# Gate rows from TensorE instead of a trip through DRAM, and a later, smaller write of the bias vectors

## The chip, the cores and the metric

The kernel runs on one core of a Trainium2 chip. The metric is the device time in microseconds (us) of one execution. Engines are named TensorE (PE in the rows; PEld is its weight load), VectorE (DVE), ScalarE (ACT), GpSimd (POOL) and SyncE (SP). A `q` behind an engine's name (ACTq, SPq) marks what its sequencer issues, DMAs above all.

## What is computed

Two layers of a decoder on 512 tokens of width 1024, float32, with a conditioning vector `c`:

```python
c_act = silu(c)
for l in range(2):
    ada = c_act @ ada_w[l] + ada_b[l]
    sh1, sc1, g1, sh2, sc2, g2 = split(ada, 6)
    h = x * (1 + sc1) + sh1
    y = even_mixer(h) if l == 0 else diff_mixer(h)    # attention; all logits get a relative-position bias
    x = layer_norm(ALPHA * x + (1 + g1) * y, ln_g[l, 0], ln_b[l, 0])
    h = x * (1 + sc2) + sh2
    y = square(relu(h @ w1[l])) @ w2[l]
    x = layer_norm(ALPHA * x + (1 + g2) * y, ln_g[l, 1], ln_b[l, 1])
```

The even mixer has eight heads of sparse attention (compressed, selected and window branches) and eight heads over a latent with a top-k selection; the odd mixer is differential attention. The relative-position bias comes from a table of 32 buckets by 16 heads and depends on the distance alone. The four vectors `1 + g1`, `1 + g2` of the two layers are what this case calls the gates.

## The kernel before

Tokens are cut into four tiles of 128, the width into eight pieces of 128. Weights come as 512 KB loads on SyncE's queue, in a fixed order, into a few raw buffers (`raw`, `early`, `s`); ScalarE casts each to a high part (L265), VectorE or GpSimd makes the low part (L266), and a product is three matmuls (L350 to L352). The instructions of every engine are put in order ahead of time by a program that goes by priority, which is the order of the code, and by its own estimate of times; an engine then runs its list in that order and waits where an input is late. PSUM has eight banks, two for each of the tags `mm`, `s`, `t` and `o`.

*Conditioning.* `adac` holds the conditioning vectors as columns (128 partitions, eight pieces). Those of the first projection come in pairs (shift and scale of piece k) from loads `ada_w` multiplied and summed on VectorE (L250) or on GpSimd and ScalarE (L247, L248).

*Gates.* A gate multiplies either the rows of an output-projection weight (L262) or the MLP's sum (L824), so it is needed as a row of 1024 repeated on 128 partitions: the tile `grow`, of which there is one buffer for all four. `gate_row(l, i)` scales the column on VectorE (L984) and calls `row` (L430), which sends the column to DRAM as a vector (L435, 1024 elements of 4 bytes) and loads it from there onto all partitions (L440, 512 KB). Both DMAs are issued by ScalarE, and the second waits for the first. Calls: for (0,0) in the loop of the sparse attention, for (0,1) in the first MLP behind the first halves of its six whole-width products (`gemm1`), for (1,0) behind the value projection of the second layer, and for (1,1) in the second MLP as in the first. Since the order of work follows what is ready, the column of (0,1) goes out while layer 0's first LayerNorm still runs (L663 is that LayerNorm's square root on ScalarE, L706 its transposes on TensorE), that of (1,0) at 631.8 us, and that of (1,1) at 779.3 us, near the end of the first MLP. There, behind it on ScalarE's queue, stands the load of `subln` (L1595, 128 floats on all partitions), a constant of the second layer that VectorE scales (L1623) between the last groups of the first MLP.

*Bias vectors.* `bias_vectors` (L587) makes, by a one-hot product, a vector of 640 biases for each of 16 heads, and a second one for the compressed branch (8 heads, 1056 values). `write` sends them to DRAM, the first in `NREP` = 35 copies of 2,560 bytes (L606, one DMA of 1400 KB), the second in 8 copies (L608, two DMAs), all on ScalarE's queue. `gtile` (L533) later reads a tile of 128 rows by 512, each row shifted by one, out of these copies (L537, SyncE's queue). The write stands in the first projection's loop over the pieces k of the width: it is issued behind the activation of piece k = 6 (L1051). That loop casts a piece's weights (L265), makes the modulated input's high and low part (L1051 to L1053) and multiplies.

Of the kernel before, what the change touches and what calls it, by code (L numbers as in the profile page):

```python
# [9 lines left out]
F32 = mybir.dt.float32  # L10
# [13 lines left out]
NVEC = 640  # L24
# [4 lines left out]
def f32(ap):  # L29
    return ap.bitcast(F32)  # L30
# [46 lines left out]
 'cp': (),  # L77
 'd4': (22, 26, 37, 46),
 'cu': {(0, 0): 3, (0, 1): 4, (0, 2): 6, (0, 3): 7, (1, 0): 16, (1, 1): 17, (1, 2): 20, (1, 3): 21}}
NREP = 35  # L80


class Part:


    def __init__(self, *tiles):
        self.tiles = tiles
# [239 lines left out]
class Trunk:  # L327
    def __init__(self, tc, a, out):
        self.tc, self.nc, self.a, self.out = tc, tc.nc, a, out
        self.lo_engine = "vector"  # L330
        self.n_rows, self.marks, self.last_max = 0, {}, None
        self.ada_tag = "mm"
        self.slotm, self.phase = {}, None
        self.sums, self.site = {}, 0
        self.st = Stream(self)
        self.gate, self.w1, self.w2, self.wp = {}, {}, {}, {}
        self.xd, self.xr = {}, {}
        self.groups = [(0, 1, 2), (3, 4, 5)] + [(f, f + 1) for f in range(6, 28, 2)] + [(28, 29, 30, 31)]
# [91 lines left out]
    def row(self, col, pool, tag, bufs=1):  # L430

        nc = self.nc
        self.n_rows += 1
        d = self.DR.tile([1024], F32, name=f"row{self.n_rows}")
        nc.scalar.dma_start(out=d.rearrange("(k p) -> p k", p=128), in_=col)  # L435
        return self.row_in(d, pool, tag, bufs)

    def row_in(self, src, pool, tag, bufs=1):
        r = pool.tile([128, 1024], F32, tag=tag, bufs=bufs, name=tag)
        self.nc.scalar.dma_start(out=r, in_=src[None, :].to_broadcast([128, 1024]))  # L440
        return r

    def proj_q(self, ps, it, c0, c1, k):
# [89 lines left out]
    def gtile(self, col):  # L533

        g = self.s2("g")
        b = self.bvec[col]
        self.nc.sync.dma_start(out=g, in_=bass.AP(tensor=b.tensor, offset=b.offset + 127,  # L537
                                                  ap=[[NVEC - 32, 4], [NVEC - 1, 32], [1, 512]]))
        return g


# [45 lines left out]
    def bias_vectors(self):  # L587
# [5 lines left out]
        for i in range(2):  # L593
            nc.scalar.dma_start(out=oh[i], in_=a["onehot"][:, HB * i:HB * i + HB])
        self.bvec = self.DR.tile([16, NREP, NVEC], F32, name="bvec")
        self.bdec = self.DR.tile([8, 8, 16 * NDEC], F32, name="bdec")
# [8 lines left out]
        def write():  # L605
            nc.scalar.dma_start(out=self.bvec, in_=sb[0][:, None, :NVEC].to_broadcast([16, NREP, NVEC]))  # L606
            for x, c in ((sb[0][:8, NVEC:], slice(0, HB - NVEC)), (sb[1][:8], slice(HB - NVEC, 16 * NDEC))):
                nc.scalar.dma_start(out=self.bdec[:, :, c], in_=x[:, None, :].to_broadcast([8, 8, x.shape[1]]))  # L608
# [181 lines left out]
    def mlp(self, l, acc, rows, last):  # L790

        nc, st = self.nc, self.st
        h1, turn = {}, [0]
        self.ada_tag = "s"

        def relu2(ps, c0, c1, hh, hl):
            r = self.z()[:, :c1 - c0]
# [232 lines left out]
    def even(self):  # L1030
        nc, a, sm, R, B, st, I = self.nc, self.a, self.sm, self.R, self.B, self.st, self.I
# [13 lines left out]
        for k in range(8):  # L1045
            st.get(I["ada", k, True])
            c2 = self.adac[:, 0, 0:16].rearrange("p (s k) -> p k s", k=8)[:, k]
            b2 = self.adab[:, 0, 0:16].rearrange("p (s k) -> p k s", k=8)[:, k]
            nc.vector.tensor_add(out=mod[:, k], in0=c2, in1=b2)
            x = xs[k].rearrange("p (t c) -> p t c", t=4)  # L1050
            act = nc.scalar.activation(out=hh[:, :, k], in_=x, func=AF.Identity, scale=mod[:, k, 1:2], bias=mod[:, k, 0:1])  # L1051
            nc.vector.tensor_scalar(out=x, in0=x, scalar1=mod[:, k, 1:2], scalar2=mod[:, k, 0:1], op0=ALU.mult, op1=ALU.add)
            nc.vector.tensor_sub(out=hl[:, :, k], in0=x, in1=f32(hh[:, :, k]))  # L1053
            w = st.get(I["b1", k])
            for n in range(4):
                self.mm3(ps1[n], [y.cols(128 * n, 128) for y in w], (hh[:, :, k], hl[:, :, k]), k == 0, k == 7)
            for t in range(4):
                self.mm3(ps1[4 + t][:, :416], (hh[:, t, k], hl[:, t, k]), [y.cols(512, 416) for y in w], k == 0, k == 7)
            st.free(I["b1", k])
            if 1 and k == 6:  # L1060
                with self.tc.issue_after(act.ins):
                    bias_write()

# [20 lines left out]
        for t in range(4):  # L1084
            ps, ts = ps1[4 + t], slice(128 * t, 128 * t + 128)
# [45 lines left out]
        due, d = {}, 1 << 30  # L1131
        for x in reversed(PLAN["ord"]):
            d = due[x] = min(d, X0 + PLAN["due"][x] if x in PLAN["due"] else d)
# [244 lines left out]
        for t in range(4):  # L1378
            ps = self.bank("mm")
# [208 lines left out]
    def odd(self):  # L1588
        nc, a, sm, R, B, C, st, I = self.nc, self.a, self.sm, self.R, self.B, self.C, self.st, self.I
# [10 lines left out]
        for half in range(2):  # L1600
            V[half] = [self.s4() if half else B.tile([128, 1024], F32, tag="u4", bufs=4, name="V") for _ in range(2)]
            for t in range(4):
# [3 lines left out]
                ps = self.bank("mm")  # L1606
# [14 lines left out]
        nc.vector.tensor_sub(out=lf[:, 2:3], in0=lf[:, 0:1], in1=lf[:, 1:2])  # L1621
        nc.vector.tensor_scalar_add(out=lf[:, 2:3], in0=lf[:, 2:3], scalar1=LAMBDA_INIT)
        nc.vector.tensor_scalar_mul(out=sub, in0=sub, scalar1=1.0 - LAMBDA_INIT)  # L1623
        self.gate_row(1, 0)
        self.mark("o")

# [295 lines left out]
```

## Time and profile before

| | |
|---|---|
| three runs | 1472.17, 1480.51, 1480.96 us; median 1480.51 |
| profiled execution | 1476.66 us, span 1474.6 us |
| mean granted TensorE clock | 0.958 of full |
| busy | TensorE 1338.9, VectorE 1144.8, ScalarE 655.6, GpSimd 577.6 us |
| DMA | 192.09 MB, of which SyncE's ring (q1) 184.67 and ScalarE's ring (q10) 5.98 |

How the rows further down are read. A timeline row has the start in us from the span's beginning, the duration in us, the engine, the line of the code, the operation with out<-in, shapes and count; brackets at its end give how long the engine had stood idle before it and what ended that. A chain row has start, duration and what the last-ending chain of work consisted of there: an engine's work, or a DMA from its issue to its landing. A row of stretches has the stretch, its length, each engine's busy time (with the number of instructions), then the granted TensorE clock, the share of time in which the 16 DMA engines were busy, and GB/s. A row of groups has line, engine, operation, shape and count, then the busy time and the mean in ns, then idle time before. A row of one line's instructions has duration as least/median/most in ns, then first and last start in us. A row of DMA rings has packets, MB and the share of the 16 engines' time in the stretch.

### The profile page before, as it was taken

The numbers are of one execution on the slowest core, as the hardware profiler recorded it, in microseconds if no ns is written. First come the engines' busy times: TensorE is split into PE (matmuls) and PEld (weight loads), VectorE is DVE, ScalarE is ACT, GpSimd is POOL, SyncE is SP. The second block draws the span as 40 slices with busy tenths as digits, with TensorE's granted clock in tenths as the row PEclk, the third lists the DMA queues.
The fourth block names the chain that finished last, engine by engine and source line by source line (L and its number), as shares of the span: only waits on it lengthen the run. The fifth ranks groups of instructions, "written<-read, shape, count | busy, mean of one in ns | idle before, by whom it ended". The sixth has DMA issues, their size and how long they took to land.

```text
span 1474.6 us, 22436 instructions
## 1 busy us (share of the span) xinstructions
PE 1338.9 (91%) x8222; PEld 1117.6 (76%) x8222; DVE 1144.8 (78%) x2185; ACT 655.6 (44%) x1404; POOL 577.6 (39%) x432
## 2 busy tenths in 40 slices
PE   6859889999879999999997799999969899999995
PEld 4738667677569888878886678887759789999974
DVE  6577898866576787878787934778965988988898
ACT  2344456746444433323332425777565433333321
POOL 2151368745441353534444531124252632222244
PEclk9969899999989999999998999999989999999997
DMA  9943433322660445373534343233341233223311
GB/s 333 232 142 117 137 101 103 130 97 72 233 185 12 172 158 207 136 205 138 208 141 103 127 171 114 93 95 100 128 149 53 72 115 112 76 99 115 113 60 58
DMA packets 63427, 192.09 MB, mean 130 GB/s; under 512 B 11875, under 2 KB 12579, under 8 KB 63317
## 3 DMA queue, kind: packets, MB, share of 16 engines
q1 hardware_dynamic: 55712, 184.67, 37.6%
q10 hardware_dynamic: 7604, 5.98, 2.0%
q8 instruction: 65, 1.06, 0.3%
q14 instruction: 46, 0.37, 0.1%
HBM read 180.52 MB, written 10.11 MB: 129 GB/s over the span
## 4 chain that ended last, share of the span: by engine, by line
PE 67%; DVE 19%; DMA 7%; issue 3%; ACT 3%; POOL 0%; DVEq 0%; ACTq 0%; SPq 0%; POOLq 0%
PE ps_mm L350 9%; PE ps_mm L351 8%; PE ps_mm L352 8%; PE ps_o L350 4%; PE ps_o L351 4%; PE ps_o L352 4%; PE ps_s L350 3%; PE ps_s L351 3%; PE ps_s L352 3%; DVE b L266 2%; PE ps_t L352 2%; PE ps_t L350 2%; PE ps_t L351 2%; DMA raw<-ev_b 2%; PE ps_s L422 2%
## 5 line engine op out<-in xcount | busy, mean ns | idle before, releaser
L350 PE MATMUL ps_mm<-hT,b 128*128 128x256 f32 (+1 forms) x560 | 190.1, 342 | 21.6 <-ACT b L265 13.2
L351 PE MATMUL ps_mm<-hT,b 128*128 128x256 f32 (+1 forms) x560 | 189.4, 339 | 5.3 <-DVE hT L717 2.7
L352 PE MATMUL ps_mm<-hT,b 128*128 128x256 f32 (+1 forms) x560 | 188.6, 338 | 1.3 <-DVE b L220 0.8
L350 PEld LDWEIGHTS ps_mm<-hT,b 128*128 128x128 f32 x560 | 108.6, 194 | 37.8 <-ACT b L265 13.2
L351 PEld LDWEIGHTS ps_mm<-hT,b 128*128 128x128 f32 x560 | 108.5, 194 | 18.4 <-DVE hT L717 3.3
L517 ACT ACTIVATE z<-z,st 128x128 f32<-128x128 f32 (+3 forms) x160 | 89.5, 560 | 66.5 <-DVE st L514 58.5
L220 POOL TENSOR_TENSOR b<-s,b 128x512 fp32r<-128x512 f32 x33 | 46.7, 1417 | 183.0 <-ACT b L219 168.9
L896 POOL TENSOR_TENSOR ot<-z,ot 128x512 fp32r<-128x512 f32 x39 | 61.7, 1583 | 141.8 <-ACT ot L895 128.2
L352 PEld LDWEIGHTS ps_mm<-hT,b 128*128 128x128 f32 x560 | 108.3, 194 | 11.7 <-DVE b L220 1.0
L350 PE MATMUL ps_o<-b,ot 128*128 128x512 f32 x251 | 101.7, 405 | 4.8 <-ACT b L265 2.4
L514 DVE CUSTOM_DVE_ANT_0 z<-ps_s,g 128x128 f32<-128x128 f32 (+3 forms) x160 | 76.1, 485 | 33.0 <-PE ps_s L505 29.2
L351 PE MATMUL ps_o<-b,ot 128*128 128x512 f32 x251 | 99.9, 398 | 0.3 <-DVE b L266 0.3
L731 DVE TENSOR_TENSOR u<-ps_o,u 128x512 f32<-128x512 f32 x121 | 82.4, 681 | 22.6 <-PE ps_o L352 22.4
L352 PE MATMUL ps_o<-b,ot 128*128 128x512 f32 x251 | 99.3, 395 | 0.0
L265 ACT CAST b<-raw 128x1024 fp32r<-128x1024 f32 (+1 forms) x62 | 64.3, 1042 | 70.6 <-issue 20.2
L265 ACT CAST b<-s 128x1024 fp32r<-128x1024 f32 x47 | 49.0, 1049 | 88.2 <-PE ps_t L351 20.5
L266 DVE TENSOR_TENSOR b<-s,b 128x1024 fp32r<-128x1024 f32 x47 | 73.9, 1576 | 17.5 <-ACT b L265 17.5
L266 DVE TENSOR_TENSOR b<-raw,b 128x1024 fp32r<-128x1024 f32 (+1 forms) x42 | 58.1, 1384 | 30.9 <-ACT b L265 30.6
L350 PE MATMUL ps_s<-b,ot 128*128 128x512 f32 x181 | 72.0, 398 | 0.0
L731 DVE TENSOR_TENSOR u<-ps_s,u 128x512 f32<-128x512 f32 x87 | 59.3, 682 | 16.0 <-PE ps_s L352 15.8
L351 PE MATMUL ps_s<-b,ot 128*128 128x512 f32 x181 | 71.1, 393 | 0.0
L352 PE MATMUL ps_s<-b,ot 128*128 128x512 f32 x181 | 70.7, 391 | 0.0
(465 smaller groups left out, 4224.4 us busy)
## 6 DMA issues: line engine op xcount, KB each, us to landing
s<-mlp_w SPq DMA_DIRECT2D x55, 512.0 KB
s<-ada_p SPq DMA_DIRECT2D x39, 512.0 KB
s<-mlp_wp SPq DMA_DIRECT2D x33, 512.0 KB
raw<-ada_w SPq DMA_DIRECT2D x23, 512.0 KB
raw<-mlp_w SPq DMA_DIRECT2D x21, 512.0 KB
raw<-mlp_wp SPq DMA_DIRECT2D x19, 512.0 KB
early<-ada_w SPq DMA_DIRECT2D x17, 512.0 KB
raw<-ada_p SPq DMA_DIRECT2D x17, 512.0 KB
```

The source lines that it names most:

```text
L220: (nc.gpsimd if PLAN["sl"][it.l][n] else nc.vector).tensor_tensor(out=lo, in0=src, in1=f32(hi), op=ALU.subtract)
L265: nc.scalar.copy(out=hi.cols(c.start, w), in_=raw[:, c])
L266: getattr(nc, ("vector", "gpsimd")[PLAN["lo"][it.name]] if it.name in PLAN["lo"] else k.lo_engine).tensor_sub(out=lo.cols(c.start, w), in0 ...
L350: mm(ps, lhsT=l[0], rhs=r[0], start=start, stop=False)
L351: mm(ps, lhsT=l[0], rhs=r[1], start=False, stop=False)
L352: mm(ps, lhsT=l[1], rhs=r[0], start=False, stop=stop)
L422: mm(ps[32 * j:32 * j + 32, :256], lhsT=self.ccol[:, 1, k:k + 1].to_broadcast([128, 32]), rhs=(r0, r1)[k // 4][:, 256 * j:256 * j + 256], ...
L514: i = nc.vector.tensor_tensor_reduce(out=z[:, :w], in0=ps, in1=bias, scale=-1.0, scalar=3e38, op0=ALU.add, op1=ALU.min, accum_out=st[:, m: ...
L517: j = nc.scalar.activation(out=z[:, :w], in_=z[:, :w], func=AF.Exp, scale=-1.0, bias=st[:, m:m + 1], accum_out=st[:, 2 + m:3 + m])
L731: self.nc.vector.tensor_add(out=u[:, sl], in0=ps, in1=u[:, sl])
L896: (nc.gpsimd if PLAN["hl"][l][f % 2] else nc.vector).tensor_tensor(out=hl[:, c0:c1], in0=r[:, c0:c1], in1=f32(hh[:, c0:c1]), op=ALU.subtract)
```

## The change

A row is made on the core: eight products per gate on TensorE, each of a gate column repeated 128 times (as the stationary operand) and the unit matrix, into two PSUM banks, and two copies by ScalarE into `grow`. Which banks are used is set by `row_tag`: `mm` in the attention stages, `t` in the MLPs. The write of the bias vectors moves from behind the activation of piece 6 to behind that of piece 7, the last one. `NREP` goes from 35 to 23, since a bias tile is now read as 8 groups of 16 rows instead of 4 groups of 32. `row_in` goes.

```diff
-NREP = 35
+NREP = 23
...
-        self.n_rows, self.marks, self.last_max = 0, {}, None
-        self.ada_tag = "mm"
+        self.marks, self.last_max = {}, None
+        self.ada_tag = self.row_tag = "mm"
...
     def row(self, col, pool, tag, bufs=1):
 
         nc = self.nc
-        self.n_rows += 1
-        d = self.DR.tile([1024], F32, name=f"row{self.n_rows}")
-        nc.scalar.dma_start(out=d.rearrange("(k p) -> p k", p=128), in_=col)
-        return self.row_in(d, pool, tag, bufs)
-
-    def row_in(self, src, pool, tag, bufs=1):
         r = pool.tile([128, 1024], F32, tag=tag, bufs=bufs, name=tag)
-        self.nc.scalar.dma_start(out=r, in_=src[None, :].to_broadcast([128, 1024]))
+        for h in range(2):
+            ps = self.bank(self.row_tag)
+            for k in range(4):
+                c = 4 * h + k
+                nc.tensor.matmul(ps[:, 128 * k:128 * k + 128], lhsT=col[:, c:c + 1].to_broadcast([128, 128]), rhs=self.ident,
+                                 start=True, stop=True)
+            nc.scalar.copy(out=r[:, 512 * h:512 * h + 512], in_=ps)
         return r
...
         self.nc.sync.dma_start(out=g, in_=bass.AP(tensor=b.tensor, offset=b.offset + 127,
-                                                  ap=[[NVEC - 32, 4], [NVEC - 1, 32], [1, 512]]))
+                                                  ap=[[NVEC - 16, 8], [NVEC - 1, 16], [1, 512]]))
...
-        self.ada_tag = "s"
+        self.ada_tag, self.row_tag = "s", "t"
...
-            if 1 and k == 6:
+            if k == 7:
                 with self.tc.issue_after(act.ins):
                     bias_write()
...
+        self.row_tag = "mm"
         self.gate_row(1, 0)
```

## Rows read from the trace of the kernel before

**Rows 1.** The page's chain that ended last, shares by engine.

```profile
PE 67%; DVE 19%; DMA 7%; issue 3%; ACT 3%; POOL 0%; DVEq 0%; ACTq 0%; SPq 0%; POOLq 0%
```

**Rows 2.** The chain in order of time, five of its transfers.

```profile
48.31 20.21 DMA raw<-ev_b
...
75.88 7.91 DMA raw<-ada_w
...
161.52 9.28 DMA raw<-ev_b
...
407.16 12.80 DMA row<-adac
...
782.37 11.58 DMA k<-subln
```

**Rows 3.** Timeline of ScalarE, 36 to 110 us.

```profile
45.54 0.68 ACTq L606 DMA_DIRECT2D bvec<-s  x1
46.25 5.62 ACTq L608 DMA_DIRECT2D bdec<-s  x2
51.98 0.97 ACT L265 CAST b<-raw 128x928 fp32r<-128x928 f32 x1 [5.63 <-issue]
...
64.90 1.04 ACT L265 CAST b<-early 128x1024 fp32r<-128x1024 f32 x1 [10.19 <-DMA early<-ev_b]
```

**Rows 4.** DMA rings from 50 to 60 us, the only one that moved.

```profile
q10 hardware_dynamic: 388, 0.99, 95.4%
```

**Rows 5.** Timelines of VectorE, TensorE and SyncE, 36 to 110 us.

```profile
48.67 0.14 DVE L1049 TENSOR_TENSOR mod<-adac,adab 128x2 f32<-128x2 f32 x1
...
54.76 0.49 PE L351 MATMUL ps_mm<-hT,b 128*128 128x512 f32 x1 [2.34 <-DVE hT L1053]
...
67.21 0.50 PE L350 MATMUL ps_mm<-hT,b 128*128 128x512 f32 x1 [2.96 <-DVE q L373]
...
47.16 0.33 SPq L134 DMA_DIRECT2D early<-ev_b  x1
...
62.24 4.73 SPq L537 DMA_DIRECT2D g<-bvec  x2
```

**Rows 6.** Timelines of ScalarE and VectorE, 146 to 170 us.

```profile
161.84 0.59 ACT L472 ACTIVATE q<-ps_mm 64x512 fp32r<-64x512 f32 x1 [8.83 <-DMA row<-adac]
...
162.46 0.69 DVE L473 SCALAR_TENSOR_TENSOR q<-ps_mm,q 64x512 fp32r<-64x512 f32 x1 [5.23 <-ACT q L472]
```

**Rows 7.** Timelines of ScalarE, VectorE and TensorE, 396 to 450 us.

```profile
420.36 0.29 ACT L663 ACTIVATE mv<-mv,eps 128x1 f32<-128x1 f32 x1 [11.63 <-DMA row<-adac]
...
413.21 0.21 DVE L659 BATCH_NORM_AGGREGATE mv<-bn 128x2 f32<-128x12 f32 x1
...
422.21 1.09 PE L706 MATMUL ps_t<-ident,ot 128*128 128x128 f32 x4 [5.50 <-DVE ot L693]
```

**Rows 8.** Timelines of ScalarE, VectorE, GpSimd and TensorE, 768 to 806 us.

```profile
779.28 0.38 ACTq L435 DMA_DIRECT2D row<-adac  x1
...
793.97 2.18 DVE L1623 TENSOR_SCALAR k<-k 128x128 f32<-128x128 f32 x1 [7.35 <-DMA k<-subln]
...
793.73 2.34 POOL L262 TENSOR_TENSOR raw<-raw,grow 128x1024 f32<-128x1024 f32 x1 [9.12 <-DMA raw<-mlp_w]
...
800.44 0.58 PE L350 MATMUL ps_t<-hT,b 128*128 128x256 f32 x1 [10.25 <-DVE z L907]
```

**Rows 9.** Busy time by stretches, 420 to 430 us.

```profile
420.00:430.00 10.00, 3.85 (x14) 2.79 (x14) 9.11 (x15) 9.64 (x21) 6.18 (x4) 0.55 0.32 102
```

**Rows 10.** Timeline of ScalarE, 1030 to 1050 us.

```profile
1045.33 0.62 ACT L517 ACTIVATE z<-z,st 128x384 f32<-128x384 f32 x1 [3.84 <-DVE st L514]
```

**Rows 11.** Timeline of TensorE, 1030 to 1050 us, and line 1685's matmuls by operand.

```profile
1040.71 0.83 PE L1685 MATMUL ps_o<-s,q 128*128 128x128 f32 x6
...
L1685 PE MATMUL ps_o<-V,q x80: 271/275/325, 919.5 to 990.3; 128*128 128x128 f32 x80
L1685 PE MATMUL ps_o<-s,q x80: 270/275/378, 995.0 to 1060.5; 128*128 128x128 f32 x80
```

**Rows 12.** Groups by form, ScalarE's copies out of PSUM.

```profile
L531 ACT COPY s<-ps_t 128x512 f32<-128x512 f32 x12 | 7.0, 580 | 6.6 <-PE ps_t L1479 6.5
```

## Prediction

> **What bounds the kernel now.** I read the chain that ended last first, because it says which engine's time counts. By shares it is TensorE's, then VectorE's, and 7% is time in which everything on the chain waits for a transfer [rows 1]. The reader is to see in it that a few transfers hold the chain far longer than their sizes explain: the row column on its way to DRAM (4 KB, 12.80 us), the small `subln` load (11.58 us), and two weight loads near the start, of which the longer takes 20.21 us [rows 2]. Then I read the timelines of the engines around each of them.
>
> *Start, 45 to 84 us.* ScalarE issues the bias write at 45.54 and 46.25; the second issue holds its queue for 5.62 us, and the cast of the last input piece (k = 7), which stands behind it, comes at 51.98 after 5.63 us of waiting [rows 3]. While the write runs it has the DMA engines to itself: from 50 to 60 us the ScalarE ring moves 0.99 MB and takes 95.4% of the engines' time [rows 4]. A weight load issued at 47.16 [rows 5] is cast only at 64.90, after a wait of 10.19 us for it [rows 3]. TensorE stands 2.34 us before 54.76 and 2.96 us before 67.21 [rows 5].
>
> *The four rows.* Each is a 4-byte scatter to DRAM followed, on the same in-order ScalarE queue, by a load that waits for it. Row (0,0): ScalarE stands 8.83 us, VectorE 5.23 us [rows 6]. Row (0,1): ScalarE stands 11.63 us and its next instruction, a LayerNorm square root whose input was there at 413.42 (413.21 + 0.21), starts at 420.36; TensorE stands 5.50 us [rows 7]. Row (1,1): its column goes out at 779.28 and ScalarE does not wait, since the load that would wait stands much later. But the `subln` load, issued behind it at 782.37, lands at 793.97, VectorE stands 7.35 us for it, a weight load on the other ring is just as late for GpSimd (9.12 us), and TensorE then stands 10.25 us [rows 2, 8]. Row (1,0) leaves no such wait on the chain.
>
> **The change part by part.**
>
> *Row (0,1).* The column's trip and the wait are gone. The square root can start at 413.42 instead of 420.36: 6.94 us, and behind it the ScalarE and VectorE work of this LayerNorm, on which TensorE depends, moves as one block. The bounds are TensorE's 5.50 us of standing still and ScalarE's 11.63 us [rows 7]. In the ten us behind it TensorE was granted 0.55 of full clock, that is for most of it the 1.2 GHz level, after it had stood still, with ScalarE busy 9.64 us and VectorE 9.11 us of the ten [rows 9]. These two keep setting the pace, so of the 3.85 us of TensorE work there, which would shrink to 3.85 x 0.55 = 2.1 at 2.4 GHz, I count 0.5 us. Together 7.4.
>
> *Row (1,1).* Without the scatter the `subln` load has nothing ahead of it, and the VectorE chain that leads to TensorE's 10.25 us wait starts 7.35 us sooner [rows 8]. Bounds: nothing, if something else made the load late, and 10.25. I take 7.4 plus 0.6 for clock regained after the shorter standstill: 8.0.
>
> *Row (0,0).* VectorE, which sets the pace in this stage, gets back 5.23 us; bounds 0 (its selection work may meet a weight load that is late anyway, as the one of 9.28 us [rows 2]) and ScalarE's 8.83 [rows 6]. The broadcast load of the row (512 KB), issued as ScalarE's wait ends, beside that weight load's 161.52, goes too, which is a reason against the lower end. I take 5.2.
>
> *Row (1,0), and the second half of row (1,1).* The broadcast of (1,1) is issued just ahead of ScalarE's instruction at 1045.33, and that one waits for VectorE and not for a transfer [rows 10]. Nothing is gained.
>
> *The bias write.* It can go once the shift and scale of k = 7 exist (48.67 + 0.14) and the activation behind them has run; with a length like the cast's 0.97 us that is 49.8, about 4.2 us later than 45.54 [rows 3, 5]. The bytes: 16 x 35 x 2,560 plus 8 x 8 x 4,224 are 1.704 MB, after it 16 x 23 x 2,560 plus the same, 1.212 MB. At the 0.99 MB in 10 us of the write alone [rows 4] that is 17.2 against 12.2 us, so it ends about 0.8 us sooner, and the first bias tile, which SyncE issues at 62.24 [rows 5] and which waits for it, is not later. What changes is who goes ahead of it. The cast of k = 7 no longer stands behind the 5.62 us issue, so TensorE's 2.34 us go; and the loads issued from 47.16 on land before the write takes the engines, so the next projection's 2.96 us go. Queued behind the write's issue on ScalarE are now the accumulation of one conditioning column and the cast of the load that was cast at 64.90; held for about 5.62 x 12.2 / 17.2 = 4.0 us, that cast comes near 55, still ahead of the end of TensorE's first projection. Late next is the conditioning weight that lands at 83.79 (75.88 + 7.91 [rows 2]): transfers fill the ring up to it, and what reaches it is the lead of the loads. So the gain lies between 0 (the same bytes, later) and 10.0, the two TensorE waits (5.3) plus the 4.73 us that two bias tiles held SyncE [rows 5]. Between them I take 4.5, near the 4.2 us by which the write is put back.
>
> *What is added.* Eight products of 128 columns in full float32 per row. The nearest rows are the attention's value products, 128 by 128 float32: eight heads with 1 + 2 + 3 + 4 of them are 80 products, and the trace has twice 80 records, so each costs two [rows 11]. Six records in 0.83 us with 0.275 for one make (0.83 - 0.275) / 5 = 0.111 each, so 16 are 0.275 + 15 x 0.111 = 1.9 us, four rows 7.7 [rows 11]. Rows (0,1), (1,0) and (1,1) fall at the head of stages in which TensorE sets the pace: 5.8. Row (0,0) falls where VectorE does: 0.7. At half clock it is twice that, the upper bound 15.5; hidden wholly, 0. ScalarE takes 2 x 0.580 us per row out of PSUM [rows 12], 4.6 us in all, beside TensorE's work; 0.5 for the banks that the next product waits for, 4.6 if that cover is gone. Together 7.0.
>
> *Sum.* 7.4 + 8.0 + 5.2 + 4.5 = 25.1, less 7.0: 18.1 us. The profiled execution took 1476.66 us (span 1474.6), so 1458.5. That execution lies 3.85 below the median of the three runs shown and between them (1472.17 to 1480.96), so I leave it unshifted.
>
> **A rule against it.** The row's own record is 12.80 us from issue to landing for 4 KB [rows 2]. The Trainium skill, "DMA: Bandwidth & Descriptors", section "Anatomy of one DMA", fits a transfer at 2.0 us plus its bytes over 436 GB/s, which for 4 KB is an estimate of 2.0 us. By that the ten us beyond it would not be the row's, and only some 2 us per waiting row would come back. Against it stands that the same delay follows two scatters with different traffic around them, and in the third place holds both rings at once [rows 2, 8].
>
> **The rivals.**
>
> 1. *The late landings have another cause.* The row waits go, since nothing waits for a scatter any more, but `subln` stays late because of what else is in flight. Then 8.0 are missing: 1466.5. For it: the other ring's weight load was as late [rows 8], so it may be traffic. Against it: it is 64 KB (128 x 128 floats) behind 4 KB on its own ring. The rule above would give about this time. Chance 0.12.
>
> 2. *The front is swallowed.* Start and row (0,0) gain nothing, because loads set the pace between them (75.88, 161.52 [rows 2]). 9.7 are missing: 1468. Chance 0.15.
>
> 3. *The front gives more.* The start gives its 10.0 and row (0,0) ScalarE's 8.83: 1458.5 - 5.5 - 3.6 = 1449.4. For it: TensorE stands still long in both stages. A bias tile's access pattern also goes from 4 outer steps to 8; the two issues that held SyncE for 4.73 us [rows 5] are what it could shorten, and they are in the 10.0. The Trainium skill's "DMA: Bandwidth & Descriptors", section "Why a DMA increments its semaphore by 16 and not by 1", says that such a pattern's slowest dimension limits how many DMA engines share a transfer; no row here shows it. Chance 0.15.
>
> 4. *The rows' banks: slower.* A row takes both PSUM banks of its tag, and they are free only when ScalarE has copied, in order behind what it waits for. If each row holds TensorE for h us more, the time is 1458.5 + 4h: above 1476.66 from h = 4.5, and with waits like ScalarE's 10.19 [rows 3] 1499. Against it: the row of the second layer comes after that layer's value projection, when the row buffer is long free, and ScalarE has no wait of that length at these places once the scatters are gone. Chance 0.08, of which 0.05 slower by over 1%.
>
> **How the numbers follow.** The forecast has 0.50; its own range is 1453 to 1464, from half of the start's span and the clock. A measurement of this kernel tells about 1% from no change, which from 1476.66 is 1461.9. Below that lie 0.8 of the forecast (0.40), rival 3 (0.15) and 0.04 of rivals 1 and 2: 0.59. Slower by over 1%: 0.05, from rival 4. The rest, 0.36, is within 1%. To leave out no more than 2 in 10 the range must take in most of rivals 1 to 3: 1446 to 1470.
>
> **What would show it.** After: no ScalarE wait over 3 us near 150 to 165 and near 405 to 425; `subln` landing within 4 us of its issue and no TensorE wait near 10 us before the last MLP group of layer 0; the cast of k = 7 ahead of the bias write's issue, and the load after it cast near 55; 64 records of float32 products for the rows at 0.11 to 0.14 us each. It is wrong if `subln` or the weight beside it is still ten us late (rival 1), if the attention stage of layer 0 starts no earlier (rival 2), or if TensorE stands in front of a product that waits for a row's copy (rival 4). The order of the instructions on each engine is laid down anew for the changed kernel by the same program; a place that comes out otherwise than before is the error I can't size from these rows.

## The result and the profile after

The changed kernel takes 1452.05 us (median of four, 1445.6 to 1455.74) against 1476.34 (median of four, 1471.34 to 1480.96): ratio 0.9845, 95% interval [0.981, 0.988]. Its profiled execution took 1449.99 us, with a span of 1448.2. On another chip, beside three experiments, the ratio was 0.9814 [0.9788, 0.984]. So it is faster by 23 to 27 us.

The chain by engine, to be read beside [rows 1]: transfers fall from 7% to 4%.

```profile
PE 67%; DVE 19%; DMA 4%; issue 4%; ACT 3%; POOL 2%; SPq 0%; DVEq 0%; ACTq 0%; POOLq 0%
```

*Start.* ScalarE's timeline, which answers [rows 3], and then the same chain in order of time, which answers the first two lines of [rows 2]:

```profile
46.43 0.97 ACT L265 CAST b<-raw 128x928 fp32r<-128x928 f32 x1 [0.48 <-DMA raw<-ev_b]
...
49.48 0.68 ACTq L606 DMA_DIRECT2D bvec<-s  x1
50.20 5.58 ACTq L608 DMA_DIRECT2D bdec<-s  x2
55.90 1.05 ACT L265 CAST b<-early 128x1024 fp32r<-128x1024 f32 x1 [5.60 <-issue]
```

```profile
49.48 11.88 DMA bvec<-s
61.38 4.04 SPq L537
66.86 9.87 DMA raw<-ada_w
```

The cast of k = 7 is 5.55 us sooner (51.98 to 46.43), and the cast that waited until 64.90 comes at 55.90. The write itself is still on the chain: SyncE's first load of a bias tile waits for it, and a conditioning weight stands behind that load.

*The rows.* Row (0,1), which answers [rows 7]: ScalarE's square root now comes 0.25 us after VectorE's statistics, and what it waits for is VectorE.

```profile
401.21 0.21 DVE L659 BATCH_NORM_AGGREGATE mv<-bn 128x2 f32<-128x12 f32 x1
...
401.46 0.30 ACT L663 ACTIVATE mv<-mv,eps 128x1 f32<-128x1 f32 x1 [5.51 <-DVE mv L659]
```

Row (1,1), which answers [rows 8]: `subln` is issued at 762.88, its user on VectorE runs at 766.94 without a wait and takes 0.21 instead of 2.18 us, and TensorE's longest wait between 755 and 800 us is 2.86 us, for a weight that VectorE splits.

```profile
762.88 0.33 ACTq L1595 DMA_DIRECT2D k<-subln  x1
...
766.94 0.21 DVE L1623 TENSOR_SCALAR k<-k 128x128 f32<-128x128 f32 x1
```

The added products, by line (duration of one: least, median, most; below it what the engine waited for in front of them, in us):

```profile
L438 PE MATMUL ps_mm<-ident,adac x32: 271/275/376, 136.6 to 863.9; 128*128 128x128 f32 x32
...
L438 PE MATMUL ps_t<-ident,adac x32: 270/275/275, 428.7 to 1095.8; 128*128 128x128 f32 x32
...
  PE ps_t L1479: 0.9, 1
  DVE ot L1549: 0.7, 1
```

```profile
862.09 2.10 PE L438 MATMUL ps_mm<-ident,adac 128*128 128x128 f32 x16
```

They are 64 records, as forecast, and the 16 of row (1,0) take 2.10 us. TensorE waited 0.9 us at most in front of any of them.

**Where the time went.** For each instruction that occurs equally often in both traces I took its start before less its start after, and the median of that in stretches of the kernel before. The lead over the kernel before, in us (P: position alone, C: copies and bias tile alone, R: rows alone; PCR is the changed kernel, first trace and second):

| stretch before | P | C | PC | R | PR | CR | PCR | PCR again |
|---|---|---|---|---|---|---|---|---|
| 100 to 125 | 14.8 | 11.8 | 15.1 | 0.9 | 8.3 | 11.0 | 15.1 | 15.9 |
| 175 to 200 | 11.2 | 9.1 | 12.4 | 7.9 | 11.9 | 16.9 | 19.1 | 20.9 |
| 300 to 325 | 6.5 | 11.2 | 7.2 | -2.8 | 8.6 | 18.6 | 13.7 | 18.1 |
| 375 to 400 | 6.8 | 9.3 | 4.5 | -2.7 | 8.7 | 18.5 | 12.0 | 13.8 |
| 425 to 450, behind row (0,1) | 9.0 | 11.3 | 5.4 | 5.2 | 15.7 | 25.4 | 20.3 | 21.1 |
| 750 to 775 | 3.9 | 12.7 | 6.1 | 4.5 | 14.6 | 24.1 | 19.5 | 20.4 |
| 800 to 825, behind row (1,1) | 9.1 | 16.4 | 10.3 | 13.4 | 23.2 | 32.7 | 28.6 | 29.1 |
| 900 to 925 | 8.6 | 17.6 | 10.3 | 9.8 | 19.9 | 29.6 | 26.1 | 27.0 |
| 1425 to 1450 | 14.0 | 15.8 | 11.4 | 10.8 | 18.3 | 31.2 | 27.7 | 30.1 |

The last two columns are one program on two chips; they differ by up to 4.4 us in this table. Kernels with the same bias edits run the same instructions in the same order on every engine up to row (0,0), near 137 us. So the row 100 to 125 has two traces of one and the same work for P and PR (14.8, 8.3), two for C and CR (11.8, 11.0) and six for both bias edits (15.1, 15.1 and 15.9 above, 12.8, 11.0 and 13.2 in the kernels further down that add something to the changed one). The pairs differ by up to 6.5 us, so a single column is good to some 5 or 6. What is too large to be that: with both bias edits the start gives 11 to 16 us, of which 4.5 is left by 375 without the rows and 12.0 and 13.8 with them; and the rows alone have nothing left at 375 of the 7.9 us they had at 175.

### The profile page after: what moved, and what is told of

It reads as the page before. It is cut to its first block, busy times and chain, and to the rows that moved or that the text cites. A ratio compares the mean times of both kernels' runs of the same rounds, so it can differ in the third digit from the quotient of the medians.

```text
span 1448.2 us, 22535 instructions
## 1 busy us (share of the span) xinstructions
PE 1342.0 (93%) x8286; PEld 1124.3 (78%) x8286; DVE 1143.5 (79%) x2185; ACT 658.8 (45%) x1412; POOL 581.0 (40%) x432
## 4 chain that ended last, share of the span: by engine, by line
PE 67%; DVE 19%; DMA 4%; issue 4%; ACT 3%; POOL 2%; SPq 0%; DVEq 0%; ACTq 0%; POOLq 0%
PE ps_mm L350 9%; PE ps_mm L351 9%; PE ps_mm L352 9%; PE ps_o L350 4%; PE ps_o L351 4%; PE ps_o L352 4%; PE ps_s L350 3%; PE ps_s L351 3%; PE ps_s L352 3%; PE ps_t L352 2%; PE ps_t L350 2%; PE ps_t L351 2%; DVE b L266 2%; PE ps_s L504 2%; PE ps_o L1297 2%
## 5 line engine op out<-in xcount | busy, mean ns | idle before, releaser
L351 PEld LDWEIGHTS ps_mm<-hT,b 128*128 128x128 f32 x560 | 108.7, 194 | 18.1 <-DVE hT L717 5.6
L517 ACT ACTIVATE z<-z,st 128x128 f32<-128x128 f32 (+3 forms) x160 | 89.3, 559 | 65.2 <-DVE st L514 56.5
L266 DVE TENSOR_TENSOR b<-s,b 128x1024 fp32r<-128x1024 f32 x47 | 70.6, 1505 | 18.7 <-ACT b L265 18.3
L265 ACT CAST b<-s 128x1024 fp32r<-128x1024 f32 x47 | 49.0, 1048 | 78.1 <-PE ps_t L351 15.8
L731 DVE TENSOR_TENSOR u<-ps_s,u 128x512 f32<-128x512 f32 x87 | 59.2, 681 | 15.8 <-PE ps_s L352 15.6
```

Of the source, the lines that this page charges most:

```text
L265: nc.scalar.copy(out=hi.cols(c.start, w), in_=raw[:, c])
L266: getattr(nc, ("vector", "gpsimd")[PLAN["lo"][it.name]] if it.name in PLAN["lo"] else k.lo_engine).tensor_sub(out=lo.cols(c.start, w), in0 ...
L351: mm(ps, lhsT=l[0], rhs=r[1], start=False, stop=False)
L517: j = nc.scalar.activation(out=z[:, :w], in_=z[:, :w], func=AF.Exp, scale=-1.0, bias=st[:, m:m + 1], accum_out=st[:, 2 + m:3 + m])
L731: self.nc.vector.tensor_add(out=u[:, sl], in0=ps, in1=u[:, sl])
```

## The experiments

All ratios are to the kernel before, run on the same chip.

| kernel | median us | before | ratio, 95% interval |
|---|---|---|---|
| P, position alone | 1464.17 | 1472.78 | 0.9944 [0.9918, 0.997] |
| C, copies and bias tile alone | 1461.57 | 1472.78 | 0.9926 [0.9898, 0.9953] |
| PC, both bias edits | 1462.26 | 1472.78 | 0.9931 [0.99, 0.9962] |
| R, rows alone | 1467.24 | 1472.78 | 0.9957 [0.9933, 0.9982] |
| PCR, the changed kernel again | 1445.99 | 1472.98 | 0.9814 [0.9788, 0.984] |
| CR, without the new position | 1446.8 | 1472.98 | 0.9825 [0.9792, 0.9857] |
| PCR with row (0,0) through DRAM | 1460.73 | 1472.98 | 0.9914 [0.9884, 0.9945] |
| PCR with unread scatters, 4-byte pieces | 1451.43 | 1472.98 | 0.9854 [0.982, 0.9888] |
| PR, 35 copies | 1450.92 | 1474.83 | 0.9851 [0.9806, 0.9897] |
| PCR with unread writes, 32-byte pieces | 1449.62 | 1474.83 | 0.9837 [0.9788, 0.9886] |
| PCR, write cut in two | 1442.59 | 1474.83 | 0.9803 [0.9751, 0.9855] |
| PCR, write behind the first projection's last activation | 1439.23 | 1474.83 | 0.9763 [0.972, 0.9806] |

### The three edits alone

My theory was that of the prediction: the parts lie in different stages and add up. Its rivals were that late landings have a cause other than the row scatters, and that the front swallows what the start gains.

**Position alone (P).**

```diff
-            if 1 and k == 6:
+            if k == 7:
                 with self.tc.issue_after(act.ins):
```

> The kernel before with one edit: the bias write stands behind the activation of the last input piece (k = 7) instead of k = 6; 35 copies and the rows through DRAM stay. Theory (the position is what the start gains by): the cast of k = 7 runs ahead of the write's issue, near 46, and TensorE's first conditioning and attention work comes 4 to 14 us sooner; at the end -4 to -12 us against before, since part may be given back behind row (0,0). Rival (the front is swallowed by later loads): the first stages are up to 5 us sooner and the end is within 3 us of before. Rival (the number of bytes is what counts): the write, 1.70 MB as before but later, makes the first bias tile about 4 us later, and the end is the same or up to +4.

Measured -8.6 us, within the theory's range and outside those of both rivals. The lead is 14.8 us at 100 and about 6.5 from 300 to 400.

**Copies alone (C).**

```diff
-NREP = 35
+NREP = 23
...
-  ap=[[NVEC - 32, 4], [NVEC - 1, 32], [1, 512]]))
+  ap=[[NVEC - 16, 8], [NVEC - 1, 16], [1, 512]]))
```

> The kernel before with one edit: 23 copies of the bias vectors instead of 35 (1.21 instead of 1.70 MB), and the bias tile read in 8 outer steps of 16 instead of 4 of 32; the write stays behind k = 6. Theory (position first, bytes second): the write's issue holds ScalarE's queue about 3.8 instead of 5.62 us and the transfer about 12 instead of 17 us, so the start is 2 to 5 us sooner and the end -2 to -5. Rival (bytes are everything, since the write holds both rings): as much as both bias edits together give, -10 to -14. Rival (swallowed): within 2 us of before.

Measured -11.2 us: my -2 to -5 is wrong. The rival's number fits, but not its reason, since the position gives nearly as much with all the bytes, and both edits together are no better than either. This edit also carries the bias tile's new pattern, and no run has the one without the other.

**Both bias edits (PC)**, the two diffs above together.

> The kernel before with both bias edits (23 copies, 8 outer steps, write behind k = 7) and the rows through DRAM. Theory: the start as in the changed kernel, first value projection and attention 10 to 15 us sooner; row (0,0)'s wait for its scatter takes some of it back, and rows (0,1) and (1,1) wait as before: -9 to -13 at the end, and together with the rows alone about the whole -24 to -27. Rival (front swallowed without the rows): within 4 us of before. Rival (the start gives all of it and the rows nothing): -20 or more.

Measured -10.5 us, as expected; the lead of 15.1 us at 100 falls to 4.5 at 375. The expectation that this and the rows make up the whole fell with the next kernel.

**Rows alone (R)**: the change's `row()`, `row_tag` and the removal of `row_in`; bias write, copies and bias tile as before.

> The kernel before with the gate rows made on TensorE, the bias write as before (35 copies, behind k = 6). Theory (the scatters of the row columns cause the late landings): no ScalarE wait near 412, the subln load lands within 4 us of its issue, VectorE's wait of 7.35 us for it is gone; -13 to -15 us at the end: about 6 at row (0,1), 8 to 9 at row (1,1), 0 to 5 at row (0,0), and some 2 us given back in the second layer by the products. Rival (late landings have another cause): subln still lands about 10 us after its issue, and the end is -5 to -7. Rival (rows gain nothing by themselves, the whole gain is the bias write's): within 3 us of before.

Measured -5.5 us: the theory's -13 to -15 is wrong, and the number is the first rival's. Yet the places where the waits stood show that the rival's reason is wrong too: no wait for `subln` is left, the lead rises by 7.9 us at row (0,1) and by 8.9 at row (1,1). What is missing is the front: +7.9 at 175 turns into -2.7 at 375. The chain of this kernel from 130 to 200 us has two weight loads in it, of which SyncE's timeline shows the second directly behind a load of a bias tile, and SyncE's waits (line, who was waited for, us in total, times, longest) show how long that one had stood:

```profile
162.70 5.42 DMA early<-ev_b
186.84 6.74 DMA early<-ev_b
```

```profile
186.20 0.55 SPq L537 DMA_DIRECT2D g<-bvec  x1
186.84 0.42 SPq L134 DMA_DIRECT2D early<-ev_b  x1
```

```profile
SPq L537 <- DVE m L1183: 10.3, 1, 10.3
```

So a bias tile waits 10.3 us for VectorE, the weight load queued behind it is late by as much, and weights are on the chain. That this is what takes the 7.9 us back is read from the trace and not tested; the order of VectorE's instructions is also another one than before from 162 us on. -10.5 and -5.5 make -16; the changed kernel has -23 to -27. The parts do not add up.

### Which pairs make the rest

**The changed kernel again (PCR).** No edit.

> The changed kernel as it is, timed again on one chip with the three kernels beside it. If the two halves of the change add up, -10.5 (both bias edits alone) and -5.5 (rows alone) make -16. If the changed kernel's first comparison (ratio 0.9845, 23 us) stands, -21 to -25, and some 7 us belong to the two halves together and to neither alone.

Measured -27.0: 11 us belong to the halves together (7 by the first comparison). In its chain between 130 and 300 us only one transfer is left among the long pieces, at 202 us:

```profile
202.49 3.45 DMA raw<-ev_out
```

**Row (0,0) alone through DRAM again.** `row_dram` is the `row` of the kernel before.

```diff
-  self.gate[l, i] = self.row(g, self.B, "grow")
+  self.gate[l, i] = (self.row if (l, i) in ((0, 1), (1, 0), (1, 1)) else self.row_dram)(g, self.B, "grow")
```

> The changed kernel, with row (0,0) alone through DRAM again. Theory (the gain at the front needs both halves: with the early start the scatter of row (0,0) makes VectorE free the bias tiles late, SyncE's weight loads stand behind the loads of bias tiles, and the stage from 150 to 300 us waits for weights): the two early<-ev_b loads are on the chain again with 5 us or more each, the lead of 14 us at 150 falls to about 5 at 375, and the end is +5 to +8 against the changed kernel. Rival (row (0,0) is worth nothing, as in the kernel with the rows alone, which was 2.7 us behind at 375): within 2 us of the changed kernel.

Measured +14.7 us against the changed kernel, twice my price. The rival (nothing, as R seemed to say) falls. The chain from 130 to 200 us has the row's trip itself in it, first the scatter, then the broadcast, and then one weight load (two had been expected).

```profile
139.03 11.18 DMA row<-adac
150.23 4.66 DMA grow<-row
162.41 4.99 DMA early<-ev_b
```

PC, which has the same trip, shows it too (11.54 and 4.74 us, then 5.35 and 5.60 for two weight loads). In the kernel before the trip ran beside weight loads that were late anyway [rows 2, 6], which may be why neither alone was worth much; no run tests that reading. The trip's price with an early start is about 9 us by the leads of PC (13.8 less 4.5 at 375) and 14 by this kernel's (13.8 less -0.3). 3.1 of these 14 are there at 100 to 125 already, ahead of the trip, so they are not the row's; and from 143 us on the order of the instructions is another one too. The time, on one chip, is the firmer figure: +14.7.

**Copies and rows without the position (CR).**

```diff
-            if k == 7:
+            if 1 and k == 6:
```

> The changed kernel with the bias write behind k = 6 again: 23 copies and the rows on TensorE, without the new position. Theory (either bias edit does most of the start's work: 11.8 us of lead at 100 from the copies alone, 14.8 from the position alone, 15.1 from both): 0 to +4 against the changed kernel, -19 to -23 against the one before. Rival (the position is what the start's gain rests on): +8 or more against the changed kernel.

+0.8 us against the changed kernel: with 23 copies and the rows on TensorE, the position is worth nothing that can be measured.

**Position and rows with 35 copies (PR).** `NREP` and the bias tile's pattern as before.

> The changed kernel with 35 copies again (1.70 MB, bias tile read in 4 outer steps): position behind k = 7 and the rows on TensorE. It fills the last of the eight combinations of position, copies and rows. Theory (either bias edit frees the start, and the rows then keep the lead): 0 to +4 against the changed kernel, -22 to -26 against the one before. Rival (the number of copies is what the front lives on, since 23 copies and rows without the position came out like the changed kernel): +6 to +14 against the changed kernel.

1450.92 us, ratio 0.9851: its interval overlaps the changed kernel's, and the medians, on different chips, are 4.9 apart: above the theory's +4 and below the rival's +6. Either bias edit does most of what both do, once the rows are off the rings: worked out from the ratios and 1473 us, the bias edits are worth 8 to 11 us without the rows, and 16 to 21 with them.

### What a scatter of 4-byte pieces does

**Unread scatters.** Nothing reads them; the rows come from TensorE.

```diff
+        d = self.DR.tile([1024], F32, name=f"row{l}{i}")
+        self.nc.scalar.dma_start(out=d.rearrange("(k p) -> p k", p=128), in_=g)
         self.gate[l, i] = self.row(g, self.B, "grow")
```

> The changed kernel, and at each of the four gate rows an added scatter of the column to DRAM (1,024 pieces of 4 bytes) on ScalarE's queue that nothing reads or waits for; the rows still come from TensorE. Theory (such a scatter holds up the transfers behind it for some 8 to 10 us): subln, issued behind it, lands 8 to 14 us after its issue again, VectorE waits 3 to 8 us for it, and the end is +5 to +10 against the changed kernel. Rival (the late landings came from other traffic): subln lands within 4 us and the end is within 2 us of the changed kernel. Rival (only what waited for the row's own data mattered): VectorE's wait for subln is under 1 us.

+5.4 us, as the theory had it (each of the four times, from 1448.84 on, is above all of the changed kernel's on that chip, up to 1446.14), and VectorE waits for `subln` again, although nothing waits for the scatter. Its timeline, and then stretches of 3 us from 765 on (after the length: busy time of TensorE, its weight loads, VectorE, ScalarE, GpSimd; last the clock, the DMA share and GB/s). The scatter is issued at 765.11, `subln` at 768.20:

```profile
776.60 0.23 DVE L1625 TENSOR_SCALAR k<-k 128x128 f32<-128x128 f32 x1 [4.26 <-DMA k<-subln]
```

```profile
768.00:771.00 3.00, 3.00 (x22) 2.73 (x21) 3.00 (x2) 1.05 (x1) 1.19 (x1) 1.00 0.08 22
771.00:774.00 3.00, 3.00 (x18) 2.60 (x18) 1.34 (x3) 0.00 (x0) 0.00 (x0) 1.00 0.27 34
774.00:777.00 3.00, 2.02 (x15) 1.68 (x13) 0.41 (x2) 0.00 (x0) 0.00 (x0) 1.00 0.63 53
777.00:780.00 3.00, 1.06 (x5) 1.06 (x6) 3.00 (x5) 0.00 (x0) 1.16 (x1) 0.80 0.73 262
```

SyncE issues a 512 KB weight load at 770.30, on the other ring:

```profile
770.30 0.33 SPq L134 DMA_DIRECT2D raw<-mlp_w  x1
```

From there to 777, with that weight and `subln` waiting, the rings move 34 to 53 GB/s. Then 262. In the stretch before that, 22 GB/s mean little, since SyncE had issued nothing since 762.84. The order of the instructions is that of the changed kernel but for one on VectorE and one that ScalarE issues, both behind 600 us. The trace lies 4.9 us behind the changed kernel's second at 100 to 125, ahead of the first added scatter, and loses another 4.7 at this place.

**The same bytes in pieces of 32.** The edit against the kernel with the unread scatters:

```diff
-        self.nc.scalar.dma_start(out=d.rearrange("(k p) -> p k", p=128), in_=g)
+        self.nc.scalar.dma_start(out=d.rearrange("(p k) -> p k", k=8), in_=g)
```

> As the kernel with the unread scatters (+5.4 against the changed kernel), but the same 4 KB go out as 128 pieces of 32 bytes instead of 1,024 of 4. Theory (the number of pieces is what holds up the queue behind): subln lands within 5 us of its issue, VectorE waits under 1 us for it, and the end is within 2 us of the changed kernel. Rival (any write to DRAM ahead on the queue does it): VectorE's wait of some 4 us for subln stays, and the end is +4 to +7.

VectorE's wait is gone, the order of the instructions is wholly that of the changed kernel, and the rings are back at 264 GB/s 3 us after `subln`'s issue at 763.16 (the weight load is issued at 765.26):

```profile
767.22 0.21 DVE L1625 TENSOR_SCALAR k<-k 128x128 f32<-128x128 f32 x1
```

```profile
763.00:766.00 3.00, 3.00 (x22) 2.73 (x21) 3.00 (x2) 1.05 (x1) 1.15 (x1) 1.00 0.10 22
766.00:769.00 3.00, 3.00 (x18) 2.60 (x17) 3.00 (x6) 0.00 (x0) 0.27 (x1) 1.00 0.82 264
```

At that place the lead over the kernel before rises by 9.1 us here, and by some 5 us less with the 4-byte scatter. The end, 1449.62 us, is +3.6 against the changed kernel on another chip, and the intervals overlap; so at this place it is the number of pieces and not the write, and for the whole time the runs leave open whether four such writes cost nothing. The Trainium skill, "DMA: Bandwidth & Descriptors", section "Rules for kernel authors", says that a last dimension that isn't contiguous lowers to one descriptor per element and should be rearranged. The two runs agree: 4.26 us of wait against none.

### Where the write could go

**The write cut in two.** 23 copies of the vectors stay behind k = 7; the two DMAs of the decay vectors go behind the last activation (line 1090) that empties the first projection.

```diff
+        def write2():
             for x, c in ((sb[0][:8, NVEC:], slice(0, HB - NVEC)), (sb[1][:8], slice(HB - NVEC, 16 * NDEC))):
...
-            nc.scalar.activation(out=gates[:, t], in_=ps[:, 384:408], func=AF.Exp, scale=-1.0)
+            act = nc.scalar.activation(out=gates[:, t], in_=ps[:, 384:408], func=AF.Exp, scale=-1.0)
+        with self.tc.issue_after(act.ins):
+            bias_write2()
```

> The changed kernel with the write of the bias vectors cut in two: the 0.94 MB that the first bias tile needs go behind k = 7, the two DMAs for the decay vectors (0.27 MB) behind the last activation that empties the first projection. Theory (the write holds the chain for 12 us, and what comes behind it on the engines sets the start): ScalarE's queue is free some 5 us sooner, the first bias tile is issued 2 to 3 us sooner, and the end is -1 to -4 against the changed kernel. Rival (the front behind it swallows a lead of this size): within 1.5 us.

1442.59 us (lowest of four 1434.2, highest 1450.32). The median is 3.4 below the changed kernel's on another chip, but the intervals overlap: unclear.

**The whole write behind that activation.** As above with `bias_write()` there, and none in the loop.

> The changed kernel with the whole write behind the last activation that empties the first projection, near 78 us; the three first loads of bias tiles come behind the conditioning weights on SyncE's queue. Theory (the loads that stand behind the write set the start, and the first use of a bias tile is near 125): the conditioning weights land near 65 instead of 77, and the first softmax comes 5 to 10 us sooner; at the end -2 to -6 if the front keeps it, 0 if it swallows it. Rival (the write only collides with later loads): the stage from 80 to 120 us loses what the one before gains, and the end is 0 to +5.

1439.23 us (lowest 1435.4, highest 1443.03), the lowest median of all: ratio 0.9763. Its interval is apart from the changed kernel's first, [0.981, 0.988], and overlaps its second, [0.9788, 0.984], a little; the two were not run beside each other. By the second it is 6.8 us below, where -2 to -6 was expected; that it is faster than the changed kernel is likely and not shown. The chain has the conditioning weight landing at 65.2 instead of 76.7 us, and SyncE takes three bias tiles at 86 us, behind the weights:

```profile
59.06 6.16 DMA raw<-ada_w
```

```profile
86.23 5.25 SPq L537 DMA_DIRECT2D g<-bvec  x3
```

The first bias tile is read at 122.5 us, so nothing needed the write as early as it stood. The lead at 100 to 125 is 18.3 us, 2.4 more than the changed kernel's on its second chip, which is less than traces of one program differ by. I expected 5 to 10 there. In the place of the bias tiles the chain now has the write's issue on ScalarE's queue, 4.85 us from 76.08, with the softmax work of line 1200 behind it; that would take back part of what the weights gain.

## Why the prediction was right, and where it wasn't

The time, 1452.05, lies in the range (1446 to 1470) and the kernel is faster by over 1%, which had the chance 0.59. But the forecast, 1458.5, is 6 us high, and the sum behind it came near for partly wrong reasons.

*Row (0,1): right.* 7.4 less 1.9 of products was forecast. The lead rises by 8.3 us at the place (7.3 in the second trace) and keeps 6.8 (5.5).

*Row (1,1): right, with one more term.* Forecast 8.0; the lead rises by 9.1 and 8.7 us. The 7.35 us of waiting are gone, and so are 1.97 us by which the instruction behind it was stretched (2.18 to 0.21). The scatter as the cause, which rival 1 denied, is shown by the added unread scatters. The estimate of 2.0 us for 4 KB, from the Trainium skill's "DMA: Bandwidth & Descriptors", section "Anatomy of one DMA", which describes transfers on GpSimd's path, is not what this row takes from ScalarE: 11.18, 11.54 and 12.80 us in three traces.

*The products: right.* 1.9 us per row were forecast; the 16 records of row (1,0) take 2.10 us, and the lead falls there by 2.5 us (2.1 in the second trace). Rival 4 had nothing to it.

*The bias write: the term that failed, 4.5 with bounds 0 to 10.* With both bias edits the start gives 11 to 16 us at 100 to 125, above the upper bound in all six traces. The sum followed the chain up to the conditioning weight that lands at 83.79, and that far it holds: the weight lands at 76.73, 7.06 us sooner. Behind it stands a chain of VectorE work that the sum did not follow. From that landing to the end of line 1099 it takes 19.7 us before and 12.6 after, 7.1 less, which makes 14.1 in all. VectorE's timeline before and after, with GpSimd's beside it:

```profile
83.80 3.36 DVE L250 SCALAR_TENSOR_TENSOR raw<-raw,cact 128x1024 f32<-128x1024 f32 x1 [3.09 <-DMA raw<-ada_w]
...
87.10 2.32 DVE L1095 TENSOR_SCALAR ss<-ss 128x4 f32<-128x4 f32 x1
...
89.45 2.33 DVE L384 TENSOR_SCALAR yi<-ss 128x4 int32<-128x4 int32 x1
...
96.10 7.42 DVE L1099 SCALAR_TENSOR_TENSOR ot<-ot,rk,g 128x128 f32<-128x128 f32 x4
...
86.04 5.71 POOL L247 TENSOR_TENSOR early<-early,cact 128x1024 f32<-128x1024 f32 x2
...
98.62 2.40 POOL L247 TENSOR_TENSOR early<-early,cact 128x1024 f32<-128x1024 f32 x1
```

```profile
76.76 1.23 DVE L250 SCALAR_TENSOR_TENSOR raw<-raw,cact 128x1024 f32<-128x1024 f32 x1 [2.29 <-DMA raw<-ada_w]
...
77.91 0.16 DVE L1095 TENSOR_SCALAR ss<-ss 128x4 f32<-128x4 f32 x1
...
78.11 0.17 DVE L384 TENSOR_SCALAR yi<-ss 128x4 int32<-128x4 int32 x1
...
86.13 3.24 DVE L1099 SCALAR_TENSOR_TENSOR ot<-ot,rk,g 128x128 f32<-128x128 f32 x4
...
79.26 4.77 POOL L247 TENSOR_TENSOR early<-early,cact 128x1024 f32<-128x1024 f32 x2 [3.06 <-DMA early<-ada_w]
```

Two instructions on 4 elements a partition take 2.3 us beside GpSimd's multiplications and 0.16 and 0.17 without them, line 1099 loses two more such stretches of 2.1 us, and line 250 takes 2.1 us less: 10.6 us between the two traces. Some 4.2 of them come back at lines 1152 and 1154 (0.41 to 2.53 and 0.34 to 2.43 us, beside the two multiplications at 79.26). The other 0.7 us is an instruction (line 485) that stands in this chain before and not after. TensorE's wait for line 1099 does not go; it comes 10 us sooner, before and after:

```profile
96.60 0.45 PE L1106 MATMUL ps_t<-ident,ot 128*128 128x128 f32 x1 [4.26 <-DVE ot L1099]
```

```profile
86.63 0.91 PE L1106 MATMUL ps_t<-ident,ot 128*128 128x128 f32 x3 [6.32 <-DVE ot L1099]
```

That late conditioning weights reach GpSimd in a burst, just where VectorE has its short chain, stands in the trace of before. The Trainium skill, "SBUF — State Buffer", section "Who interferes with whom", says that some instructions of VectorE contend with GpSimd for a shared pair of ports, which one of them can hold for a whole instruction. The trace agrees: each stretched instruction of these small ones ends within 0.25 us of the end of a GpSimd instruction.

*Row (0,0): the other term that failed, 5.2 with an upper end of 8.83.* It was priced from its wait in the kernel before. With the late start the lead at 375 us shows nothing of it (R: -2.7, within what traces differ by); with the early start its return costs 14.7 us of time. Its price hangs on the start.

*What the sum lacked is that the terms depend on each other.* Rival 2, the front is swallowed, is in part what happens to each half alone. Rival 3, the front gives more, is nearest to the time (1449.4), but not by its reason: it adds two waits in place, where the halves are worth 7 to 11 us more together than one by one. Two obstacles in a row, of which the second sets the pace when the first is gone, fit the chains; they are not shown to be the whole of it.

*The order laid down anew, the error I named, is there, and the traces show it.* The two traces of the changed kernel have one order on every engine. The order of the kernel before is another one from 46 us on. Its SyncE takes both first bias tiles (62.24 [rows 5]) ahead of three conditioning weights; the changed kernel's takes one weight ahead of them and one between them. SyncE before and after:

```profile
68.40 0.34 SPq L134 DMA_DIRECT2D early<-ada_w  x1
...
70.94 5.26 SPq L134 DMA_DIRECT2D raw<-ada_w  x2
```

```profile
59.45 1.71 SPq L134 DMA_DIRECT2D early<-ada_w  x1
...
61.38 4.04 SPq L537 DMA_DIRECT2D g<-bvec  x1
65.52 0.63 SPq L134 DMA_DIRECT2D raw<-ada_w  x1
66.20 0.60 SPq L537 DMA_DIRECT2D g<-bvec  x1
66.86 0.47 SPq L134 DMA_DIRECT2D raw<-ada_w  x1
```

With the copies alone the tiles still go ahead of those weights, and the lead is 11.8 us all the same, so the order of these loads can't be most of it. But every edit to the bias write or to row (0,0)'s trip brought its own order with it, and no run holds the order fixed. How much of the start's gain, and of what the halves are worth together, comes from the order stays open. The unread scatters don't have this doubt.

*What would show it.* The cast of k = 7 ahead of the write, the next one near 55 (55.90), no ScalarE wait over 3 us at row (0,0), no `subln` wait, no TensorE wait near 10 us before the last MLP group: all there; the records follow each other at 0.13 us (2.10 for 16), within the 0.11 to 0.14 named. At row (0,1) a wait over 3 us is left (5.51), but for VectorE.

## What to carry to other kernels

Two late things in front of one stage are to be priced together: here each gave less alone (-10.5 and -5.5 us) than the pair gave (-23 to -27). A transfer's price is what it does to the transfers behind it, on either ring: count its pieces before its bytes. And follow a late load to the instruction at which everybody waits again, with the engines that it sends to work at the same moment, before an upper bound is set. Where a program lays down the order of the instructions, compare the order in the two traces before a gain is put down to the edit.

## What the hardware showed that I had not expected

- With 1,024 pieces of 4 bytes under way, both rings together moved 34 to 53 GB/s for about 7 us while `subln` and a 512 KB weight were waiting; with the same bytes as 128 pieces of 32 they were at 264 GB/s 3 us after `subln`'s issue.
- Two instructions on VectorE that take 0.16 and 0.17 us took 2.32 and 2.33 us beside GpSimd's 128x1024 multiplications, each to the end of the one beside it.
- A write of 0.94 MB in 23 copies, with 0.27 MB behind it, held the chain for 11.88 us, though the first instruction that reads a bias tile ran 66 us after it had landed (127.2 us): what needed it was the queue in which the tile's load stood.
